# A gated-delta recurrence with raw keys: key norms and beta as row factors of the decay matrices, the values and the last product

## The chip, the cores and the metric

The kernel runs on one core of a Trainium2 chip. Its time is the device time of one execution in microseconds; before the change it is 2602.99 us, the median of three runs (2598.48 to 2603.35). One core has five engines that run side by side, each with its own queue of instructions worked off in order: TensorE (PE; its weight loads are listed apart as PEld), VectorE (DVE), ScalarE (ACT), GpSimd (POOL) and SyncE (SP), which here only issues DMA transfers.

## The reference

One layer of a streaming encoder is computed for 2048 prompt frames and for 8 running streams of 16 frames, all of width 1024. Each stream of tokens goes through a normalization, a wide projection, two head groups side by side, an output projection and a gated feed-forward part. The change lies in group A, the gated delta rule with 4 heads of 128:

```
q = l2norm(silu(conv(q))) * 128 ** -0.5
k = l2norm(silu(conv(k)))            # l2norm(x) = x * rsqrt(sum(x * x) + EPS)
v = silu(conv(v))
beta = sigmoid(b),   g = -exp(A_log) * softplus(a + dt_bias),   G = cumsum(g) inside a chunk
A    = strict_lower((beta_i k_i . k_j) * exp(G_i - G_j))
u, w = solve (I + A) [u | w] = [beta v | beta k exp(G)]
v_new = u - w S
o     = (q exp(G)) S + (lower(q . k) * exp(G_i - G_j)) v_new
S     = S * exp(G_last) + (k exp(G_last - G))^T v_new
```

`o` is normalized by head afterwards and gated with SiLU(z). All of it is float32.

## The kernel before

The tokens are 17 tiles of 128: 16 of the prompt, each of which is one chunk of the recurrence, and one (tile 16) that holds the 8 sample streams. They go through the first phase in six groups of two or three tiles:

```
GROUPS = [[0, 1, 16], [2, 3, 4], [5, 6, 7], [8, 9, 10], [11, 12], [13, 14, 15]]
```

The later phases (output projection, feed-forward) work on all tiles again and are not touched. For each group the first phase does, in program order: `x_prep` (rows normalized, split into a rounded part `hi` and a remainder `lo`; `x_first` for the first group); `gate_prep` (b and a projected; from them `sb`, `eG`, `tl`, `eL` and per tile the decay matrix `dt`); `qkv_stage`; `pair_stage`; `level_stage`; `z_stage`; one `chunk_stage` per prompt tile (`sample_stage` for tile 16); `sc_stage` (head group B).

A projection (`project`, line 352) of one block of 128 channels is 24 matmuls of 128x128 by 128x384 into one PSUM bank of the `psd` pool: 8 blocks of the contraction times three products of hi and lo parts (`mm3`, line 139). Its weights come by `fetch` and `weights`: in the first group they are cast on ScalarE (342) and the remainder is made by GpSimd or VectorE (344); later they are mostly read back, already split, as 1 MB transfers.

In `qkv_stage` the projections come out channel-major. `conv_qkv` moves the bank to SBUF (374 or 376), makes the four taps (401 or 403 on ScalarE, 370 on VectorE) and applies SiLU (405, 407). Then, per head:

- Keys: the tile is transposed to token-major in a bank of the `pst` pool, which has two (427); ScalarE squares and sums each row (412); `rstd` makes the inverse norm with a VectorE operation (131) and a power on GpSimd (133); VectorE multiplies it by `sb`, the square root of beta (430), and scales the keys with it while it copies them out of the bank (431), into `kt`. `kt` is then transposed back to channel-major in another `pst` bank (435) and copied by ScalarE into `kT` (437). So `kt` and `kT` both hold sqrt(beta) k / |k|.
- Values: transposed (444) and scaled by `sb` on the way out of the bank (445), into `vt`.
- Queries: `qT` is the channel-major SiLU itself; a transposition (452) only serves to sum the squares `ssq`, with which `out_stage` corrects the normalization of the output.

`pair_stage` forms k^T k and k^T q per head (519, 520) and multiplies both by `dt` (523 into `AU`, 524 in place into `dt`, from then on named QK). `AU` is written to memory in blocks of 32 and the 32x32 triangles are inverted by 31 steps of two VectorE operations each (539, 541); `level_stage` merges the blocks into `U`, the inverse for the 128 rows. `chunk_stage` forms the right-hand side from `kT`, the state, `eG` and `vt` (625 to 628), multiplies by `U` (632) into `yt`, scales `kt` by `tl` on GpSimd (636), and updates state (639, 642) and output (646 to 652).

Nothing of the order is written out by hand: a planner, which models the time of every instruction, writes the order of each engine's queue. Work of one group's recurrence is interleaved with the projections of the next. The tiles `kT`, `qT`, `kt`, `vt` lie in two pools that the groups use in turn; `kraw` and `vraw` share a ring of three buffers.

## Time and profile before

| | before |
|---|---|
| median of three runs | 2602.99 us |
| profiled execution, its own time | 2609.88 us |
| its span | 2608.1 us |
| granted TensorE clock, mean | 0.987 |
| busy in the span: PE, PEld, DVE, ACT, POOL | 2509.2, 2337.4, 1748.9, 1033.2, 645.1 us |
| instructions | 41962 |

A profile is one execution. Its busy times are sums over an engine's instructions; matmuls overlap, so TensorE's busy time is not its limit. Rows of groups give line, engine, operation, output and inputs with their shapes, the count, then the busy time in us and the mean in ns of one, and after the second bar the idle time of the engine just before them and what ended it. The chain of waits is followed back from the last instruction: at each step to what released it, or to the instruction before it on its engine. Rows of stretches give the busy time of each engine in a part of the span.

### The profile page before, as it was taken

Reading aid. Unit: us, or ns where it says so; the run is one execution under the profiler, and the core shown is the slowest. Engines: PE = TensorE matmul, PEld = TensorE weight load, DVE = VectorE, ACT = ScalarE, POOL = GpSimd, SP = SyncE. Lnnn points to the kernel's source line nnn. Section 1 sums busy time; section 2 is a strip of 40 time slices with the busy share of each in tenths; the row PEclk is TensorE's granted clock in tenths of the full one; section 3 lists DMA queues with packets and bytes.
Section 4 is the critical chain, followed back from the end, with each engine's and each line's share of the span. In section 5 each row is a group of like instructions: output and inputs, shape, how many; then the busy total and the mean of one; then the engine's idle time right before and its main releaser. Section 6 shows DMA issues by size and latency. Waiting matters only on the chain.

```text
span 2608.1 us, 41962 instructions
## 1 busy us (share of the span) xinstructions
PE 2509.2 (96%) x15129; PEld 2337.4 (90%) x15129; DVE 1748.9 (67%) x3549; ACT 1033.2 (40%) x2496; POOL 645.1 (25%) x598
## 2 busy tenths in 40 slices
PE   8989999999989999999999999999999999999998
PEld 7989899999888988778999999999999988788786
DVE  7787766666587665777878864544655555677598
ACT  6545144261554423444434442222433335333343
POOL 3321101010120101214556620000000025555563
PEclk9999999999999999999999999999999999999999
DMA  7876575757567573768877788887988853443466
GB/s 266 297 267 238 193 268 198 246 193 237 193 205 247 184 233 129 234 216 287 291 253 271 264 281 259 280 246 244 295 272 296 275 176 106 125 125 122 128 216 185
DMA packets 320816, 589.42 MB, mean 226 GB/s; under 512 B 55533, under 2 KB 204721, under 8 KB 301793
## 3 DMA queue, kind: packets, MB, share of 16 engines
q1 hardware_dynamic: 182512, 509.28, 58.8%
q10 hardware_dynamic: 138096, 77.46, 9.8%
q8 instruction: 120, 1.97, 0.3%
q14 instruction: 88, 0.71, 0.1%
HBM read 424.60 MB, written 162.05 MB: 225 GB/s over the span
## 4 chain that ended last, share of the span: by engine, by line
PE 70%; DVE 11%; DMA 9%; ACT 4%; issue 3%; POOL 2%; ACTq 1%; SPq 0%; DVEq 0%; POOLq 0%
PE fbank L1010 32%; PE dbank L139 15%; PE fbank L1168 10%; PE tbank L794 3%; PE dbank L794 3%; DMA xk<-in_xT 1%; DVE xr L1187 1%; DMA dr<-in_w_dn 1%; DVE acc L370 1%; DMA xt<-in_x 1%; DVE acc L1127 1%; DMA w<-wsplit 1%; DVE Ts L541 1%; DMA partd<-pt 1%; DMA utd<-sT 1%
## 5 line engine op out<-in xcount | busy, mean ns | idle before, releaser
L1010 PE MATMUL fbank<-xh,fw 128*128 128x384 f32 (+1 forms) x3696 | 901.3, 327 | 9.4 <-ACT m L1044 4.4
L139 PE MATMUL dbank<-hi,w 128*128 128x384 f32 (+1 forms) x2688 | 685.3, 334 | 12.7 <-ACT w L342 6.0
L1010 PEld LDWEIGHTS fbank<-xh,fw 128*128 128x128 f32 x3696 | 653.2, 188 | 11.3 <-ACT m L1044 5.0
L1010 PE MATMUL fbank<-xl,fw 128*128 128x384 f32 (+1 forms) x1848 | 603.7, 327 | 0.0
L139 PEld LDWEIGHTS dbank<-hi,w 128*128 128x128 f32 x2688 | 480.8, 191 | 18.5 <-ACT w L342 6.0
L1168 PE MATMUL fbank<-dw,as 128*128 128x512 f32 x1980 | 458.8, 393 | 8.6 <-DVE acc L1127 2.5
L1168 PEld LDWEIGHTS fbank<-dw,as 128*128 128x128 f32 x1980 | 370.6, 188 | 96.5 <-DVE acc L1127 4.5
L139 PE MATMUL dbank<-lo,w 128*128 128x384 f32 (+1 forms) x1344 | 446.4, 332 | 1.1 <-DVE lo L228 1.1
L1010 PEld LDWEIGHTS fbank<-xl,fw 128*128 128x128 f32 x1848 | 348.1, 188 | 0.0
L139 PEld LDWEIGHTS dbank<-lo,w 128*128 128x128 f32 x1344 | 256.9, 191 | 3.7 <-DVE lo L228 1.7
L1152 POOL TENSOR_TENSOR as<-ar,as 128x256 fp32r<-128x256 f32 (+1 forms) x207 | 186.5, 911 | 277.7 <-ACT as L1149 276.9
L1127 DVE TENSOR_TENSOR acc<-acc,fbank 128x512 f32<-128x512 f32 x248 | 166.3, 682 | 93.4 <-PE fbank L1168 75.6
L867 POOL TENSOR_TENSOR dw<-dr,dw 128x512 fp32r<-128x512 f32 x52 | 77.3, 1498 | 484.6 <-ACT dw L865 484.4
L1149 ACT CAST as<-ar 128x256 fp32r<-128x256 f32 (+1 forms) x288 | 117.8, 427 | 181.3 <-PE fbank L1168 130.0
L985 ACT CAST fw<-rg 128x512 fp32r<-128x512 f32 x124 | 77.3, 623 | 188.9 <-PE fbank L1010 170.8
L370 DVE SCALAR_TENSOR_TENSOR acc<-R,cw,acc 128x384 f32<-128x384 f32 (+2 forms) x216 | 132.8, 620 | 12.8 <-ACT acc L401 8.8
L344 POOL TENSOR_TENSOR w<-wr,w 128x512 fp32r<-128x512 f32 x49 | 73.0, 1490 | 228.0 <-ACT w L342 170.5
L1057 DVE TENSOR_TENSOR c<-u,fbank 128x384 f32<-128x384 f32 (+1 forms) x66 | 34.9, 529 | 102.2 <-PE fbank L1010 102.0
L1053 DVE TENSOR_TENSOR m<-m,m 128x384 f32<-128x384 f32 (+1 forms) x44 | 23.1, 525 | 97.8 <-ACT m L1046 97.8
L539 DVE TENSOR_TENSOR pr<-As,Ts 48x31 f32<-48x31 f32 (+25 forms) x186 | 66.7, 359 | 29.8 <-DMA As<-sa 25.7
L342 ACT CAST w<-wr 128x512 fp32r<-128x512 f32 x98 | 56.4, 616 | 61.9 <-PE dbank L139 29.4
L1055 ACT ACTIVATE m<-fbank 128x384 f32<-128x384 f32 (+1 forms) x66 | 31.2, 473 | 121.5 <-PE fbank L1010 112.4
(358 smaller groups left out, 3708.3 us busy)
## 6 DMA issues: line engine op xcount, KB each, us to landing
w<-wsplit SPq DMA_DIRECT2D x119, 1024.0 KB, 5.3
fw<-fsplit SPq DMA_DIRECT2D x188, 512.0 KB, 4.8
fsplit<-fw SPq DMA_DIRECT2D x94, 512.0 KB, 4.0
partd<-pt ACTq DMA_DIRECT2D x88, 384.0 KB, 6.5
rg<-in_w_gu SPq DMA_DIRECT2D x62, 512.0 KB, 4.3
wsplit<-w SPq DMA_DIRECT2D x28, 1024.0 KB, 5.3
wr<-in_w_in SPq DMA_DIRECT2D x98, 256.0 KB, 3.9
ar<-partd SPq DMA_DIRECT2D x48, 384.0 KB, 3.3
```

What stands on the lines that cost most here:

```text
L139: T.matmul(ps, l, r, start=(i == 0), stop=(i == n - 1))
L344: e.tensor_tensor(out=wl[:, c], in0=wr, in1=wh[:, c].bitcast(F32), op=ALU.subtract)
L370: V.scalar_tensor_tensor(acc, raw(d), w[:, d:d + 1], acc, op0=ALU.mult, op1=ALU.add)
L539: V.tensor_mul(p3, As[:m, j, j + 1:32].unsqueeze(2).broadcast_to([m, a, b]), Ts[:m, j, 0:b].unsqueeze(1).broadcast_to([m, a, b]))
L794: T.matmul(pss[n], m_[:, j, :], w_[k][:, n * 512:(n + 1) * 512], start=(k == 0 and ci == 0), stop=(k == KD - 1 and ci == 2))
L867: e.tensor_tensor(out=w[:, 1], in0=v, in1=w[:, 0].bitcast(F32), op=ALU.subtract)
L985: A.copy(w[:, 0], v)
L1010: T.matmul(ps, w_[:, c], b_[k][:, :hw], start=(first and k == 0 and ci == 0), stop=(k == KH - 1 and ci == 2), skip_group_check=not first)
L1127: V.tensor_add(dst, dst, ps)
L1149: ins = A.copy(a[:, 0, :n], v)
L1152: e.tensor_tensor(out=a[:, 1, :n], in0=v, in1=a[:, 0, :n].bitcast(F32), op=ALU.subtract)
L1168: T.matmul(ps, a[:, x_, q * P:(q + 1) * P], w[:, y_], start=(start and q == 0 and ci == 0), stop=(q == c - 1 and ci == 2), skip_group_chec ...
```

## The change

The inverse norms and beta are taken out of the keys. With s = sum of squares + EPS, the kernel now works with raw keys after SiLU:

- `kT` is the channel-major SiLU output itself (written straight into the pool's tile instead of the ring), and `kt` is its transposition, copied out of the bank by ScalarE. The second transposition, the `rstd` of each key head and its two multiplications by VectorE go.
- The sums of squares of all four heads are collected in one tile `ssk`, and once per group `c2` = beta / s is made on VectorE and `rt` = s ** 0.5 by one power on GpSimd (with a constant 0.5 in a new tile `half`).
- `beta` is now exp(-softplus(-b)) where `sb` was its square root (scale -1.0 instead of -0.5 in line 285).
- The values are scaled by `rt` instead of `sb` (same instruction and shape).
- `tl`, the factors of `kt` in the last product, is multiplied by `c2` (one operation per group).
- Each decay matrix `dt` is multiplied per head by the column of `c2` of its tile on ScalarE: four multiplications of 128x128 per tile, placed after a value head.

`sumsq` now writes into a tile that is handed to it.

```diff
--- before.py
+++ after.py
@@ -125,6 +125,8 @@
     g_hd = vec[:, 16:17]
     neghalf = const.tile([P, 4 * MAXT], F32, name="neghalf")
     V.memset(neghalf, -0.5)
+    half = const.tile([P, 4 * MAXT], F32, name="half")
+    V.memset(half, 0.5)
 
     def rstd(small, ss, n, scale, eps, tag):
         m = small.tile([P, n], F32, tag=tag + "m", name=tag + "m")
@@ -282,7 +284,7 @@
             sp3 = sp.rearrange("p (t c) -> p t c", c=8)
             sb, gg, nG, eG, tl, eL = (sm(nm) for nm in ("sb", "gg", "nG", "eG", "tl", "eL"))
             v3 = lambda a: a.rearrange("p (t h) -> p t h", h=H)
-            A.activation(v3(sb)[:, :n], sp3[:, :n, 0:4], AF.Exp, scale=-0.5)
+            A.activation(v3(sb)[:, :n], sp3[:, :n, 0:4], AF.Exp, scale=-1.0)
             V.tensor_mul(v3(gg)[:, :n], sp3[:, :n, 4:8], nega.unsqueeze(1).broadcast_to([P, n, H]))
             ps = bank() if rb is not None else tbank()
             q = 4 * npr
@@ -321,7 +323,7 @@
                                            neg_s if t == SAMPLE else neg_p, op0=ALU.add, op1=ALU.add)
                 A.activation(dt, dt, AF.Exp)
                 dts.append(dt)
-            return dict(sb=sb, eG=eG, tl=tl, eL=eL, eLs=eLs, dt=dts)
+            return dict(beta=sb, eG=eG, tl=tl, eL=eL, eLs=eLs, dt=dts)
 
         wloads = []
         stores = []
@@ -406,36 +408,35 @@
             if npr < n:
                 A.activation(dst[:, pc:c].rearrange("p (s l) -> p s l", s=NS), segments(acc, pc, 0, 3 + LS)[:, :, 3:], AF.Silu)
 
-        def sumsq(ps, n, nm):
-            ss = small.tile([P, n], F32, tag=nm, name=nm)
+        def sumsq(ps, n, ss):
             for i in range(n):
-                A.activation(junkq, ps[:, i * P:(i + 1) * P], AF.Square, accum_out=ss[:, i:i + 1])
-            return ss
+                A.activation(junkq, ps[:, i * P:(i + 1) * P], AF.Square, accum_out=ss(i))
 
         def qkv_stage(tiles, hi, lo, rb, gt, pool):
             n = len(tiles)
             c = n * P
+            m = 4 * n
             kt = pool.tile([P, H, MAXT, P], F32, tag="kt", name="kt")
             vt = pool.tile([P, H, MAXT, P], F32, tag="vt", name="vt")
+            ssk = small.tile([P, 4 * MAXT], F32, tag="ssk", name="ssk")
             kT, qT, ssq = [], [], []
-            sb = gt["sb"].rearrange("p (t h) -> p t h", h=H)
             for h in range(H):
-                raw = cp.tile([P, W1], F32, tag="kvT", name="kraw", bufs=NKV)
-                conv_qkv(tiles, 4 + h, project(h, hi, lo, c), raw, rb)
+                o = pool.tile([P, W1], F32, tag="kT", name="kT", bufs=H)
+                conv_qkv(tiles, 4 + h, project(h, hi, lo, c), o, rb)
                 ps = tbank()
                 for i in range(n):
-                    T.transpose(ps[:, i * P:(i + 1) * P], raw[:, i * P:(i + 1) * P], ident)
-                ss = sumsq(ps, n, "ssk")
-                rk = rstd(small, ss, n, 1.0, EPS, "rk")
-                V.tensor_mul(rk, rk, sb[:, :n, h])
-                V.tensor_mul(kt[:, h, :n], ps[:, :c].rearrange("p (t d) -> p t d", d=P),
-                             rk.unsqueeze(2).broadcast_to([P, n, P]))
-                ps = tbank()
-                for i in range(n):
-                    T.transpose(ps[:, i * P:(i + 1) * P], kt[:, h, i, :], ident)
-                o = pool.tile([P, W1], F32, tag="kT", name="kT", bufs=H)
-                A.copy(o[:, :c], ps[:, :c])
+                    T.transpose(ps[:, i * P:(i + 1) * P], o[:, i * P:(i + 1) * P], ident)
+                sumsq(ps, n, lambda i: ssk[:, 4 * i + h:4 * i + h + 1])
+                A.copy(kt[:, h, :n], ps[:, :c].rearrange("p (t d) -> p t d", d=P))
                 kT.append(o)
+            c2 = small.tile([P, 4 * MAXT], F32, tag="c2", name="c2")
+            rt = small.tile([P, 4 * MAXT], F32, tag="rt", name="rt")
+            V.tensor_scalar_add(ssk[:, :m], ssk[:, :m], EPS)
+            G.tensor_tensor(out=rt[:, :m], in0=ssk[:, :m], in1=half[:, :m], op=ALU.pow)
+            V.reciprocal(c2[:, :m], ssk[:, :m])
+            V.tensor_mul(c2[:, :m], c2[:, :m], gt["beta"][:, :m])
+            V.tensor_mul(gt["tl"][:, :m], gt["tl"][:, :m], c2[:, :m])
+            rt3 = rt.rearrange("p (t h) -> p t h", h=H)
             for h in range(H):
                 raw = cp.tile([P, W1], F32, tag="kvT", name="vraw", bufs=NKV)
                 conv_qkv(tiles, 8 + h, project(4 + h, hi, lo, c), raw, rb)
@@ -443,14 +444,19 @@
                 for i in range(n):
                     T.transpose(ps[:, i * P:(i + 1) * P], raw[:, i * P:(i + 1) * P], ident)
                 V.tensor_mul(vt[:, h, :n], ps[:, :c].rearrange("p (t d) -> p t d", d=P),
-                             sb[:, :n, h].unsqueeze(2).broadcast_to([P, n, P]))
+                             rt3[:, :n, h].unsqueeze(2).broadcast_to([P, n, P]))
+                if h < n:
+                    for g in range(H):
+                        A.mul(gt["dt"][h][:, g, :], gt["dt"][h][:, g, :], c2[:, 4 * h + g:4 * h + g + 1])
             for h in range(H):
                 o = pool.tile([P, W1], F32, tag="qT", name="qT", bufs=H)
                 conv_qkv(tiles, h, project(8 + h, hi, lo, c), o, rb)
                 ps = tbank()
                 for i in range(n):
                     T.transpose(ps[:, i * P:(i + 1) * P], o[:, i * P:(i + 1) * P], ident)
-                ssq.append(sumsq(ps, n, f"ssq{h}"))
+                ss = small.tile([P, MAXT], F32, tag=f"ssq{h}", name=f"ssq{h}")
+                sumsq(ps, n, lambda i: ss[:, i:i + 1])
+                ssq.append(ss)
                 qT.append(o)
             gt.update(kt=kt, vt=vt, kT=kT, qT=qT, ssq=ssq)
 
```

## The prediction

> **What bounds the kernel now.** I read the page first, then the stretches of 25 us, then TensorE's waits, and the single instructions last.
>
> ```profile
> span 2608.1 us, 41962 instructions
> PE 2509.2 (96%) x15129; PEld 2337.4 (90%) x15129; DVE 1748.9 (67%) x3549; ACT 1033.2 (40%) x2496; POOL 645.1 (25%) x598
> ```
> ```profile
> PE 70%; DVE 11%; DMA 9%; ACT 4%; issue 3%; POOL 2%; ACTq 1%; SPq 0%; DVEq 0%; POOLq 0%
> ```
>
> TensorE is busy 96% of the span and carries 70% of the chain that ended last. So an instruction taken off TensorE is worth its time, and one taken off another engine is worth only the wait that it ends. The edit lies in the recurrence's phase, so the stretches of that phase come next. The columns are the stretch, its length, the busy time of PE, PEld, DVE, ACT and POOL (with counts), the granted clock, the DMA share and GB/s.
>
> ```profile
> 0.00:1050.00 1050.00, 989.86 (x6937) 933.35 (x6937) 711.47 (x1892) 454.21 (x1212) 153.43 (x156) 0.98 0.67 224
> ```
> ```profile
> 150.00:175.00 25.00, 16.84 (x82) 15.11 (x82) 21.45 (x61) 6.13 (x12) 6.16 (x5) 0.80 0.91 310
> 175.00:200.00 25.00, 25.00 (x240) 22.78 (x239) 15.55 (x48) 21.83 (x48) 2.70 (x4) 1.00 0.57 212
> ...
> 400.00:425.00 25.00, 24.70 (x168) 24.23 (x168) 18.68 (x55) 14.53 (x44) 5.00 (x5) 1.00 0.62 208
> ```
>
> In the first 1050 us TensorE is idle for 1050 - 989.9 = 60 us. The worst stretch is the handover from the first group to the second (16.8 of 25 busy). Where key and value heads of a later group run (400 to 425) TensorE is full, while ScalarE has 25 - 14.5 = 10.5 us free and the DMA share is 0.62, so neither sets the pace there. TensorE's waits in this phase, with the total, the times and the longest:
>
> ```profile
> PE tbank L139 <- ACT hi L209: 12.0, 4, 8.0
> ...
> PE tbank L435 <- DVE kt L431: 4.3, 6, 2.5
> PE tbank L452 <- ACT junkq L412: 3.6, 3, 2.2
> ```
>
> The second row is the transposition that the edit removes: it waits for the normalized keys.
>
> **The change part by part.** *Term A, the transpositions.* Line 435 goes, 68 of them (17 tiles by 4 heads).
>
> ```profile
> L435 PE MATMUL tbank<-cst,kt 128*128 128x128 f32 x68 | 12.3, 276 | 4.3 <-DVE kt L431 4.3
> ```
> ```profile
> 169.44 1.92 PE dbank L139 x6
> ...
> 187.10 4.39 PE dbank L139 x24
> ...
> 211.01 0.33 PE tbank L435 x3
> ```
>
> One takes 276 ns, but they overlap: in the chain three of them take 0.33 us, 0.11 each. The lower price is 68 x 0.11 = 7.5 us; the upper is the 12.3 us of busy time, which contains the pipeline's tails that other matmuls overlap. I take 7.5, because the chain counts each stretch of time once.
>
> *Term B, their waits.* The 4.3 us before line 435 go with it if nothing else is late at the same place, and stay whole if the next instruction is. Next in line is the transposition of another head's keys or values, which after the edit waits only for a SiLU and for a transposition bank. That bank is freed sooner too: by the three squares and a copy, without the way over VectorE, GpSimd and VectorE again. Of 0 to 4.3 I take 3.
>
> *Term C, the handover from the first group to the second.* These rows are from the timelines of TensorE, ScalarE and VectorE.
>
> ```profile
> 93.08 0.52 PE L435 MATMUL tbank<-cst,kt 128*128 128x128 f32 x3 [0.18 <-DVE kt L431]
> ```
> ```profile
> 92.23 0.42 ACT L405 ACTIVATE qT<-acc 128x256 f32<-128x256 f32 x1 [1.24 <-DVE acc L370]
> ```
> ```profile
> 164.52 0.18 DVE L541 TENSOR_TENSOR Ts<-Ts,pr 48x31 f32<-48x31 f32 x1
> ...
> 166.10 1.01 DVE L206 TENSOR_TENSOR xk<-xk,rb 128x384 f32<-128x384 f32 x2
> ```
>
> The last head's keys are transposed again only at 93.1, and the pair matrices need all heads. The long solve on VectorE that comes out of them ends at 164.7, and the next group's rows follow at 166.1, for which TensorE waits 8.0 us. The edit lets the keys through earlier and takes about 4 us of work from VectorE in each group (below), but the last queries get their SiLU at 92.2 as well, so the pair matrices can't come much sooner. The bounds are 0 and 8.0 plus the slow start behind the wait: six matmuls of line 139 take 1.92 us there (0.32 each), 24 take 4.39 later (0.18 each). If 6 to 8 of them ran slow, that is 6 to 8 x 0.14 = about 1, so 9 us. I take 2, near the lower end, because the queries are as late as the keys.
>
> [...]
>
> *Term D, VectorE and GpSimd.*
>
> ```profile
> L431 DVE TENSOR_TENSOR kt<-tbank,rkr 128x384 f32<-128x384 f32 (+1 forms) x24 | 12.7, 531 | 0.3
> L430 DVE TENSOR_TENSOR rkr<-rkr,sb 128x3 f32<-128x3 f32 (+1 forms) x24 | 6.8, 285 | 5.1 <-POOL rkr L133 4.7
> L131 DVE TENSOR_SCALAR rkm<-ssk 128x3 f32<-128x3 f32 (+1 forms) x24 | 5.0, 209 | 12.0 <-ACT junkq L412 12.0
> ...
> L278 DVE RECIPROCAL ru<-uu 128x24 f32<-128x24 f32 (+1 forms) x6 | 1.7, 286 | 0.0
> L307 DVE TENSOR_TENSOR tl<-tbank,nG 128x12 f32<-128x12 f32 (+1 forms) x5 | 0.8, 168 | 5.6 <-ACT eL L306 5.6
> ```
> ```profile
> L133 POOL TENSOR_TENSOR rkr<-rkm,neghalf 128x3 f32<-128x3 f32 (+1 forms) x24 | 23.5, 979 | 120.4 <-DVE rkm L131 98.4 <-DVE R L391 13.7 <-DVE hist L393 8.2
> ```
>
> VectorE loses 12.7 + 6.8 + 5.0 = 24.5 us and gets per group a reciprocal (0.29) and three small operations (0.17 each): 6 x 0.8 = 4.8. GpSimd does 6 powers instead of 24: 23.5 becomes about 6. Neither is the bound, so D is 0 beyond what C holds; the added clearing of a small constant lies ahead of all this and is 0 too.
>
> *Term E, ScalarE.* The copy of the second transposition (line 437) becomes a copy of the first, the same in number and shape: 0. New are 68 multiplications of 128x128 by a column; no row shows one in SBUF. The nearest rows:
>
> ```profile
> L412 ACT ACTIVATE junkq<-tbank 128x128 bf16<-128x128 f32 x136 | 37.4, 275 | 37.2 <-PE tbank L452 15.2 <-DVE o L652 5.8 <-PE dbank L139 3.6
> ...
> L401 ACT ACTIVATE acc<-dbank,cw 128x384 f32<-128x384 f32 x48 | 28.2, 587 | 0.1
> ...
> L437 ACT COPY kT<-tbank 128x384 f32<-128x384 f32 x20 | 9.5, 473 | 10.5 <-PE tbank L435 10.3
> ```
>
> The shape alone gives 275 ns. A column factor adds 587 - 473 = 114, so 389 is the upper price: 18.7 to 26.5 us in all, and 12 x 0.39 = 4.7 in a group of three tiles. I take the upper one, as the operand is a column. The cover is ScalarE's 10.5 us of idle time per 25 in those stages. On the path I put 1 us for it, out of 0 to 26.5. Queued behind a multiplication on ScalarE are the evacuations and SiLUs of the next heads, for which VectorE's taps and TensorE's banks wait; it has itself only the squares and two or three small VectorE operations to wait for, and the exponentials that were made earlier on the same engine.
>
> *Term F, the new wait.* The values are now multiplied by the key norms, so the first of them waits for all four key heads and for the one power. In the third group:
>
> ```profile
> 409.94 0.33 PE tbank L427 x3
> ...
> 420.57 0.33 PE tbank L444 x3
> ```
>
> The last keys are transposed 10.6 us before the first values. Three squares (0.8), their reads (no more than that again), an addition (0.2) and a power (1.0) take 2.8 us at most, so the wait is covered by nearly 8 us. That cover is gone if the power stands in GpSimd's queue behind a blocked product of the recurrence:
>
> ```profile
> POOL kl L636 <- PE gbank L639: 52.7, 9, 15.2
> ```
>
> Its longest wait is 15.2 us; behind that, the values would come 15.2 + 2.8 - 10.6 = 7.4 us late, less the time that the second bank gives (one projection, 4.4 by the 24 matmuls above): about 3 us in a group, 15 in five. I take 0.
>
> *The sum.* 7.5 + 3 + 2 - 1 = 11.5 us. The profiled execution took 2609.88 us (span 2608.1 and 1.8 around it), so it would be 2598.4. The median of the three runs is 2602.99, 6.9 below the profiled one; taken off the median, the forecast is 2591.5. Unknown beyond this is the planner: it writes every engine's order anew from modelled times. The trace bounds its luck by what the same handover costs in different places: 8.0 us once, (12.0 - 8.0) / 3 = 1.3 on average elsewhere, so up to about 6.
>
> **The rivals.** *Larger:* B and C come whole. 7.5 + 4.3 + 9 = 20.8, 2582. For it speaks that keys leave the first group's late chain; against it that the queries stay. *No change:* the freed time comes back as waits, above all term F, or as a handover made worse by the planner's 6 us: 11.5 less 6 to 15, about 2600. For it speaks the row of line 636; against it that GpSimd has less to do and the values lie 10 us behind. *Slower:* ScalarE becomes the bound around the values and queries. Place: the multiplications stand ahead of the next heads' evacuations and SiLUs. It decides where ScalarE has less than 4.7 us free in its stretch, that is above about 20 of 25, as at 175 to 200 (21.8). Price: up to 26.5 on the path against 7.5 + 3 + 2 = 12.5, so up to +14; at three quarters, 19.9 - 12.5 = +7, 2610. Against it: in the key and value stage above it stands at 14.5. [...] *Not what it says* is hard to see: the diff drops lines 434 and 435 outright.
>
> **How the numbers follow.** The forecast has 0.60, its own range 2583 to 2597 (the sum at 20 to 6); the larger gain 0.10; no change 0.17; slower 0.13. About 0.2%, 5 us, is what a measurement can tell from no change. So faster is 0.60 + 0.10 = 0.70, same 0.17, slower 0.13. The range is 2579 (the larger gain and 3 us of the planner's) to 2606: it takes in no change and leaves out most of slower.
>
> **What would show it.** Right: no row of line 435, TensorE's matmuls fewer by 68, VectorE's busy time about 20 us lower, GpSimd's 17, ScalarE's some 20 to 26 higher; TensorE's idle time in the first 1050 us lower by a few us. Wrong: waits of the value transpositions for their scaled product or of that product for the power (F); of TensorE for ScalarE's evacuations in the value and query stages (E); a longer wait for the next group's rows (C or the planner).

## The result, and the profile after

The changed kernel takes 2627.35 us (median of four runs, 2621.65 to 2629.62); the kernel before takes 2603.17 us (median of four runs, 2598.48 to 2605.61; three of them are the runs of the table at the start). The ratio is 1.0075, with a 95% interval of 1.0049 to 1.0100. The forecast was a gain of 11.5 us; the kernel became about 20 us slower by the ratio (24 by the two medians), and the time lies above the range. Beside the experiments below the kernel before took 2607.7 to 2611.4 us; set against these, the 2627.35 us of the change are 0.6 to 0.75% slower.

First the page of the changed kernel: the span, the busy times of the engines, and the shares of the chain that ended last. (These add up to 58%: the chain was followed no further back, and does not reach the recurrence.)

```profile
span 2625.3 us, 41826 instructions
PE 2518.9 (96%) x15061; PEld 2345.7 (89%) x15061; DVE 1744.6 (66%) x3502; ACT 1057.0 (40%) x2567; POOL 632.9 (24%) x580
PE 46%; DVE 6%; DMA 2%; issue 2%; POOL 1%; ACT 1%; ACTq 0%; SPq 0%; DVEq 0%; POOLq 0%
```

TensorE has 15061 matmuls where it had 15129: exactly 68 fewer. Yet its busy time went *up*, from 2509.2 to 2518.9 us. Fewer instructions with more busy time means that some of those that stayed ran slower. The granted clock says the same (view of the cores, first the kernel before, then the changed one):

```profile
core 0: 2608.1 us, clock 0.987
```
```profile
core 0: 2625.3 us, clock 0.979
```

In the records of both kernels this clock has only two values, 1 and 0.5. So the time at half clock is twice what is missing to 1: 2 x 0.013 x 2608.1 = 68 us before, 2 x 0.021 x 2625.3 = 110 us after, 42 us more. The profiled execution of the changed kernel has the lowest clock of its four (the others 0.981 to 0.983), so the 42 us are rather too much than too little.

Where in the program? The source view of the first matmul line of the feed-forward part (the same matmuls, line 1010 before and 1016 after; the columns are count, ns of one at three quantiles, and first start to last) gives the length of all that lies ahead of it:

```profile
L1010 PE MATMUL fbank<-xh,fw x3696: 303/334/522, 1198.9 to 2128.0; 128*128 128x384 f32 x130, 128*128 128x320 f32 x65
```
```profile
L1016 PE MATMUL fbank<-xh,fw x3696: 302/334/689, 1214.4 to 2144.2; 128*128 128x384 f32 x130, 128*128 128x320 f32 x65
```

It starts 1214.4 - 1198.9 = 15.5 us later, and the span ends 17.2 us later. So nearly all of the loss arises ahead of the feed-forward part. The stretches of the changed kernel there (length, then busy time of PE, PEld, DVE, ACT, POOL with counts, clock, DMA share, GB/s):

```profile
0.00:1050.00 1050.00, 985.24 (x6809) 930.51 (x6810) 699.03 (x1839) 477.91 (x1282) 141.99 (x137) 0.97 0.65 222
50.00:75.00 25.00, 22.15 (x113) 21.31 (x114) 17.35 (x46) 19.36 (x51) 8.47 (x6) 0.80 0.58 198
975.00:1000.00 25.00, 21.41 (x134) 18.46 (x131) 16.11 (x29) 12.08 (x21) 2.48 (x2) 0.74 0.64 211
```

Both of the 25 us stretches had a full clock before, the first of them the one in which the first group's keys and values run:

```profile
50.00:75.00 25.00, 21.91 (x133) 20.95 (x132) 19.16 (x56) 17.42 (x44) 8.62 (x7) 1.00 0.78 265
...
975.00:1000.00 25.00, 25.00 (x137) 21.32 (x136) 18.64 (x36) 11.98 (x26) 4.61 (x4) 1.00 0.59 180
```

After, TensorE is as busy at 50 to 75 us (22.2 against 21.9) but gets through 113 matmuls instead of 133, at a clock of 0.80. In neither stretch is another engine busy throughout (at most 19.4 of 25 us), so it isn't seen there that one of them became the bound for good. Shorter stretches of the changed kernel show how the clock falls:

```profile
49.50:52.90 3.40, 1.88 (x15) 1.88 (x15) 1.25 (x5) 3.35 (x10) 1.27 (x1) 1.00 0.01 2
52.90:56.30 3.40, 2.58 (x9) 1.98 (x9) 2.84 (x9) 3.36 (x10) 0.00 (x0) 0.50 0.70 255
56.30:59.70 3.40, 2.39 (x9) 2.39 (x10) 0.98 (x5) 3.29 (x15) 1.09 (x1) 0.50 0.57 207
59.70:63.10 3.40, 3.40 (x13) 3.30 (x12) 1.85 (x6) 2.70 (x7) 2.47 (x2) 0.50 0.00 0
```
```profile
51.02 0.55 PE L428 MATMUL tbank<-cst,kT 128*128 128x128 f32 x3 [1.73 <-ACT kt L430]
...
57.31 0.90 PE L445 MATMUL tbank<-cst,vraw 128*128 128x128 f32 x3 [1.55 <-ACT kt L430]
```

In the second view, TensorE's timeline, a number in square brackets is the wait ahead of an instruction, with what ended it. TensorE is kept waiting 1.73 us before a key transposition and 1.55 us before a value transposition, both times for the copy of a key head out of its bank, which stands in a ScalarE that is full (3.35 of 3.4 us). The clock falls after the first of the two waits and is 0.5 from 52.9 to 63.1 us; the second wait lies inside.

To say what share each of these has, I reckon every kernel of this case in the same way, from its TensorE records. Each matmul is given as *work* the usual distance from its start to the next start (the 30th percentile of its line and shape over all runs). *Gaps* is the time from its end to the next start. What remains inside the stretches at half clock is the *half-clock loss*, what remains elsewhere the *rest*; some 19 us at the two ends belong to none. The level of the half-clock loss depends by about 6 us on how the matmuls are grouped for their usual distance (another grouping gives 22.3 and 38.4 us for the two kernels below), the difference of two kernels by one to three. In microseconds of the profiled execution:

| | work | gaps | half-clock loss | rest | span |
|---|---|---|---|---|---|
| before | 2420.9 | 80.3 | 28.0 | 60.0 | 2608.1 |
| after | 2412.8 | 87.6 | 45.0 | 60.7 | 2625.3 |
| difference | -8.1 | +7.3 | +17.0 | +0.7 | +17.2 |

The 8 us of the transpositions are gained, as forecast. About the same amount comes back as gaps, and 17 us more are lost because TensorE runs 42 us longer at half clock.

### The profile page after: what moved, and what is told of

Its sections match the earlier page's. It is cut to its first block, busy times and chain, and to the rows that moved or that the text cites. A ratio compares the mean times of both kernels' runs of the same rounds, so it can differ in the third digit from the quotient of the medians.

```text
span 2625.3 us, 41826 instructions
## 1 busy us (share of the span) xinstructions
PE 2518.9 (96%) x15061; PEld 2345.7 (89%) x15061; DVE 1744.6 (66%) x3502; ACT 1057.0 (40%) x2567; POOL 632.9 (24%) x580
## 4 chain that ended last, share of the span: by engine, by line
PE 46%; DVE 6%; DMA 2%; issue 2%; POOL 1%; ACT 1%; ACTq 0%; SPq 0%; DVEq 0%; POOLq 0%
PE fbank L1016 33%; PE fbank L1174 11%; PE tbank L800 1%; PE dbank L800 1%; DVE xr L1193 1%; DVE acc L1133 1%; DMA partd<-pt 1%; POOL dw L873 1%; DMA dr<-in_w_dn 1%; DVE as L1158 0%; DMA fh<-hTd 0%; DVE dw L873 0%; DVE acc L1190 0%; DVE xl L944 0%; DVE fw L992 0%
## 5 line engine op out<-in xcount | busy, mean ns | idle before, releaser
L873 POOL TENSOR_TENSOR dw<-dr,dw 128x512 fp32r<-128x512 f32 x52 | 76.8, 1490 | 486.0 <-ACT dw L871 485.7
L545 DVE TENSOR_TENSOR pr<-As,Ts 48x31 f32<-48x31 f32 (+25 forms) x186 | 63.6, 342 | 26.4 <-DMA As<-sa 22.1
```

The lines of the kernel that those rows point to most:

```text
L545: V.tensor_mul(p3, As[:m, j, j + 1:32].unsqueeze(2).broadcast_to([m, a, b]), Ts[:m, j, 0:b].unsqueeze(1).broadcast_to([m, a, b]))
L873: e.tensor_tensor(out=w[:, 1], in0=v, in1=w[:, 0].bitcast(F32), op=ALU.subtract)
```

## The experiments

**Three theories.** *S*: the load that the change adds on ScalarE (68 multiplications, and the copies of the keys that wait behind them) holds up TensorE's banks; without it the kernel would be faster than before. *P*: the planner writes all orders anew after any edit; the order it had found for the kernel before falls well, those for the changed kernel fall worse, and the edit's own work hardly matters. *C*, which goes with either: short gaps cost more than their length, because a stretch of short gaps and tiny matmuls brings the clock down, as it seems to from 52.9 us above (1.88 of 3.4 us busy, no gap longer than 1.73 us, then a clock of 0.50).

Each experiment gives a ratio to the kernel before with its 95% interval and the terms of the same reckoning.

### Without the multiplications, and with nothing but them

The first leaves out the multiplications of the decay matrices by `c2` (in the changed kernel they are line 450) and puts a constant -5 into the masks in their place, so that the numbers stay in a similar size; part of the computation is left out. The second adds the same 68 multiplications, by a column of ones, to the kernel before.

```diff
 # e1_no_scale, against the changed kernel
-                if h < n:
-                    for g in range(H):
-                        A.mul(gt["dt"][h][:, g, :], gt["dt"][h][:, g, :], c2[:, 4 * h + g:4 * h + g + 1])
 # e2_before_plus_scale, against the kernel before
+                if h < n:
+                    for g in range(H):
+                        A.mul(gt["dt"][h][:, g, :], gt["dt"][h][:, g, :], ones[:, 4 * h + g:4 * h + g + 1])
```

> The changed kernel without the 68 multiplications of the decay matrices on ScalarE (line 443 of it). It leaves the factors beta / |k|^2 out of the decay matrices; a constant of -5 in the exponent's mask keeps the solve bounded, with the same instructions. Theory S (ScalarE's new work is the burden): most of the 24 us comes back, so 2600 to 2608, and TensorE's time at half clock falls from 108 us towards the 67 us of the kernel before. Theory P (the planner writes a new order for any edit, and how its gaps fall is luck): the time may go either way by some 10 us, with no relation to ScalarE's busy time; near 2620 is as likely as 2600. Theory C (small gaps in TensorE's work cost double, since they halve its clock for the windows behind them) says only that time follows matmul work plus gaps plus the loss at half clock, in this run as in the others.

> The kernel before with 68 multiplications of the decay matrices on ScalarE added behind its value heads, at the same place as in the change, by a column of ones, so that the output stays the same. Theory S: slower by most of the change's loss plus what the transpositions saved, some 20 to 32 us, so 2623 to 2635. Theory P: anything from -10 to +15 us, about 2593 to 2618, and the same size as for an edit without weight.

| | ratio [95%] | work | gaps | half-clock loss | span |
|---|---|---|---|---|---|
| e1_no_scale | 1.0024 [1.0012, 1.0036] | 2412.5 | 88.6 | 37.2 | 2617.5 |
| e2_before_plus_scale | 1.0028 [1.0012, 1.0044] | 2420.9 | 85.9 | 40.3 | 2625.1 |

Without the multiplications the changed kernel is still slower than before, with the gaps of the whole change (88.6 against 87.6 us). With them alone the kernel before loses 0.28%. Together that is 0.52%, less than the 0.75% of the change. The median of e2, 2618.19 us, lies below the 2623 to 2635 us that S said; its profiled execution, 2626.85 us, is the slowest of seven, so the row shows it at its worst. But e1 is what speaks most against S: the kernel with 68 matmuls and 47 VectorE instructions fewer and nothing on ScalarE but squares and copies as before is 0.24% slower.

### The keys' copy on VectorE; the second transposition gone alone

In e3 the changed kernel's copy of the transposed keys is VectorE's instead of ScalarE's. In e4 the kernel before loses its second transposition and nothing else: the raw keys serve as `kT`, without a factor (computation left out; -5 in the masks and in `tl` in place of the factors), while norms, `kt`, values and queries stay as they were.

```diff
 # e3_kt_dve
-                A.copy(kt[:, h, :n], ps[:, :c].rearrange("p (t d) -> p t d", d=P))
+                V.tensor_copy(kt[:, h, :n], ps[:, :c].rearrange("p (t d) -> p t d", d=P))
 # e4_before_no_second
-                raw = cp.tile([P, W1], F32, tag="kvT", name="kraw", bufs=NKV)
+                raw = pool.tile([P, W1], F32, tag="kT", name="kT", bufs=H)
...
-                ps = tbank()
-                for i in range(n):
-                    T.transpose(ps[:, i * P:(i + 1) * P], kt[:, h, i, :], ident)
-                o = pool.tile([P, W1], F32, tag="kT", name="kT", bufs=H)
-                A.copy(o[:, :c], ps[:, :c])
-                kT.append(o)
+                kT.append(raw)
```

> The changed kernel with the copy of the token-major keys out of the bank on VectorE, as before, in place of ScalarE. Theory S (ScalarE's load): the copies (11 us) leave ScalarE, the two waits of TensorE for that copy in the first group go, and the time falls by a few us, to about 2615 to 2622 beside 2627. Theory P (the planner's order decides, and with it where gaps and half-clock windows fall): anything between 2605 and 2630. Theory C (time follows matmul work plus gaps plus loss at half clock) has to hold in the trace either way.

> The kernel before with the second transposition and its copy alone left out: the channel-major keys stay raw, the token-major ones are normalized as before. What it leaves out is the norm and beta in one of the two copies of the keys; two constants of -5 in exponents keep the numbers bounded, with as many instructions. It has the saving of the change and none of its additions, and ScalarE has 11 us less to do. The prediction's terms A and B: 7.5 to 11.8 us faster, 2591 to 2596. Theory P: the 8 us of matmul time are saved for certain, but gaps and half clock move by luck, so 2580 to 2610, and a time above 2603 would speak for it alone.

| | ratio [95%] | work | gaps | half-clock loss | span |
|---|---|---|---|---|---|
| e3_kt_dve | 1.0033 [1.0020, 1.0047] | 2413.5 | 87.1 | 39.0 | 2617.0 |
| e4_before_no_second | 1.0030 [1.0018, 1.0042] | 2413.6 | 82.9 | 40.4 | 2612.1 |

e4 is the purest form of the idea: work is taken away and none is put in its place. It gets its 7.3 us of work (2420.9 to 2413.6) and is 0.30% slower all the same, through 12.4 us more of half clock in its profile (gaps +2.6, the rest -3.6). In its waits of TensorE in the first 1050 us (total, times, longest) there is no line of a key transposition any more:

```profile
PE dbank L139 <- DMA w<-wsplit: 8.1, 7, 2.4
PE tbank L139 <- ACT hi L209: 8.0, 1, 8.0
PE tbank L179 <- DVE rg L176: 7.4, 2, 6.8
```

Other waits stand there, and the order is another one. Compared by the sequence of source lines on TensorE ahead of the feed-forward part, e4's order matches that of the kernel before in a share of 0.51, the changed kernel's in 0.48. Such a share depends on the way of matching (others give 0.55 to 0.78 for the kernels compared here), so only its distance from 1 is used.

The copy on ScalarE, that ended the two waits shown above, isn't the only cause of the lost clock in the first group: e3 has no such copy and e4 no ScalarE work that was not there before, and a half-clock stretch stands at 57 to 64 us in the one and at 54 to 61 in the other. The time of e3 (2616.89 us) decides nothing, as it lies in what S said, 2615 to 2622 us, and in what P said.

### The same work elsewhere

Three kernels move the multiplications of the changed kernel: to GpSimd (e7) and to VectorE (e8), one instruction per tile instead of four, and, in a_fold, into the exponent, where nothing is multiplied: the logarithm of `c2` is added to `nG` and the decay matrices are made after the key heads.

```diff
 # e7_scale_pool (e8_scale_dve: V.tensor_mul with the same operands)
-                    for g in range(H):
-                        A.mul(gt["dt"][h][:, g, :], gt["dt"][h][:, g, :], c2[:, 4 * h + g:4 * h + g + 1])
+                    G.tensor_tensor(out=gt["dt"][h], in0=gt["dt"][h], in1=bc(c2[:, 4 * h:4 * h + 4]), op=ALU.mult)
 # a_fold
+            A.activation(lc[:, :m], c2[:, :m], AF.Ln)
+            V.tensor_add(gt["nG"][:, :m], gt["nG"][:, :m], lc[:, :m])
+            gt["decay"]()
```

> The changed kernel with the decay matrices scaled by GpSimd, one instruction of 128x512 per tile (17 in all, about 1.15 us each by the row of line 636), in place of 68 on ScalarE. Theory S: ScalarE falls back by its 20 to 26 us, and the time to that of the run without the scaling, about 8 us above the kernel before in the same call, unless VectorE is held up by it. Theory P: anything within 10 us of that.

> The same with the scaling on VectorE, 17 instructions of 128x512, about 0.75 us each by the row of line 612, 13 us in all. Theory S: like the run with GpSimd, since VectorE still has less to do than before; about 6 to 10 us above the kernel before. Theory P: anything within 10 us of that.

> The changed kernel without the 68 multiplications: the logarithm of beta / |k|^2 is added to the column that goes into the exponent of the decay matrices, which are made after the key heads (one logarithm and one addition of 128x12 per group). Nothing is left out of the computation. Theory S: as the run without the scaling, 0.24% above the kernel before, less if its order is kind. Theory P: 0 to 0.7% above, without relation to ScalarE.

| multiplications on | ratio [95%] | gaps | half-clock loss | span |
|---|---|---|---|---|
| ScalarE, 68 (the change) | 1.0075 [1.0049, 1.0100] | 87.6 | 45.0 | 2625.3 |
| GpSimd, 17 (e7) | 1.0063 [1.0045, 1.0082] | 93.8 | 35.8 | 2621.0 |
| VectorE, 17 (e8) | 1.0045 [1.0028, 1.0062] | 90.3 | 40.5 | 2621.4 |
| none, in the exponent (a_fold) | 1.0063 [1.0047, 1.0079] | 87.9 | 42.8 | 2623.0 |
| none, left out (e1) | 1.0024 [1.0012, 1.0036] | 88.6 | 37.2 | 2617.5 |

The groups of instructions give their price, in the changed kernel, in e7 and in e8 (busy time, ns of one, then idle time ahead):

```profile
L450 ACT ACTIVATE dt<-dt,c 128x128 f32<-128x128 f32 x68 | 20.8, 388 | 0.2 <-DVE c L437 0.2
```
```profile
L449 POOL TENSOR_TENSOR dt<-dt,c 128x512 f32<-128x512 f32 x17 | 19.1, 1142 | 5.8 <-DMA xt<-in_x 4.4 <-ACT dt L324 1.4
```
```profile
L449 DVE TENSOR_TENSOR dt<-dt,c 128x512 f32<-128x512 f32 x17 | 13.1, 806 | 0.0
```

From 20.8 us on ScalarE to nothing on any engine, the ratios show no relation with the load: a_fold, which multiplies nothing, is as slow as e7 and within the interval of the change. S had put a_fold at the 0.24% of e1, and e7 and e8 at about 6 to 10 us above the kernel before, where they lie at some 16 and 12; it falls. What all five share is raw keys, and orders that are not that of the kernel before.

### Edits without work

If P holds, an edit that does nothing should move the time as well. e5 clears 12 columns on VectorE once per group in the kernel before, e6 copies 12 columns on ScalarE; nobody reads the result.

```diff
+            nop = small.tile([P, 12], F32, tag="nop", name="nop")
+            V.memset(nop, 0.0)              # e5_before_dve_nop
+            A.copy(nop, ones[:, 0:12])      # e6_before_act_nop
```

> The kernel before with one VectorE memset of 128x12 more in each of the six groups, about 0.1 us each and read by nobody. Theory S: no change, within 2 us of 2603. Theory P: the planner's order differs and the time with it, by 5 us or more in one of the two directions, with gaps and half-clock time moved by as much.

> The kernel before with one ScalarE copy of 128x12 more in each of the six groups (about 0.2 us each), read by nobody. Theory S: no change, within 2 us of the kernel before. Theory P: as VectorE's idle instruction gave no change, this one tells whether a small edit on ScalarE, whose order decides when banks are free, does: 5 us or more either way if it does.

e5: 0.9998 [0.9989, 1.0007]; e6: 1.0003 [0.9988, 1.0018]. No change, which looked like a blow to P. But the order on TensorE matches that of the kernel before in a share of 0.997 and 0.993: the planner put the small instructions in and left all else. The two runs show that an edit without effect on the order has none on the time, and nothing on what another order costs. They also show how far two executions of nearly one order differ in the reckoning: e5 has 80.1 us of gaps, e6 75.8, and half-clock losses some 4 and 5 us below that of the kernel before. Smaller differences in these tables say nothing.

So two exchanges followed that do the same work in another order, made alike in the kernel before (b) and in the changed one (a). In *qv* the query heads come before the value heads, with the weights' order to match; in *zl*, `z_stage` comes before `level_stage` in the loop over the groups.

```diff
 # b_qv, a_qv: query loop ahead of the value loop, and
-        order = [(j, gi) for gi in range(len(GROUPS)) for j in range(28)]
+        order = [(j, gi) for gi in range(len(GROUPS)) for j in (*range(4), *range(8, 12), *range(4, 8), *range(12, 28))]
 # b_zl, a_zl: the call of level_stage moves behind that of z_stage
-            level_stage(tiles, gt)
...
+            level_stage(tiles, gt)
```

> The kernel before with the four query heads ahead of the four value heads in each group (order of the weights and of the stage alike). No instruction is added or removed, but the planner's order on TensorE differs widely, which it did not with the two idle instructions. Theory P (the order of the kernel before falls well, and any edit that gives another order loses that): slower by 0.2 to 0.7%, with the matmul work as before and the loss at half clock up by 8 to 17 us. Theory S (the change pays for work that it adds): within 0.2% of the kernel before.

> The changed kernel with the query heads ahead of the value heads. Theory P: about as far above or below the changed kernel's 0.75% as luck has it, 0 to 0.8% above the kernel before, and within 0.4% of the kernel before with the same exchange. Theory S: 0.5 to 0.8% above the kernel before with the same exchange; the value transpositions, which wait for the key norms, come later, so that wait (the prediction's term F) can't be what costs.

> The kernel before with the z stage's four projections ahead of the level stage in program order; again no instruction added or removed and another order on TensorE. Theory P: slower by 0.2 to 0.7% through gaps and half clock. Theory S: within 0.2%.

> The changed kernel with the same exchange of z stage and level stage. Theory P: 0 to 0.8% above the kernel before, within 0.4% of the kernel before with that exchange. Theory S: 0.5 to 0.8% above the kernel before with that exchange.

| | ratio [95%] | work | gaps | half-clock loss | span |
|---|---|---|---|---|---|
| b_qv | 1.0063 [1.0041, 1.0086] | 2421.7 | 93.7 | 35.7 | 2626.6 |
| a_qv | 1.0062 [1.0043, 1.0081] | 2412.9 | 94.1 | 40.6 | 2625.0 |
| b_zl | 1.0013 [1.0000, 1.0026] | 2421.5 | 83.9 | 29.7 | 2612.6 |
| a_zl | 1.0026 [1.0012, 1.0040] | 2413.3 | 90.4 | 34.2 | 2615.3 |

b_qv computes what the kernel before computes, with the same number of matmuls, and loses 0.63%: 13.4 us more of gaps and 7.7 of half clock. Its order matches in a share of 0.57, that of b_zl in 0.51. With *qv* the kernels with and without the change are equal (1.0063 and 1.0062); with *zl* they differ by 0.13%, where S had put the changed one 0.5 to 0.8% above the other in both. For b_zl itself P missed: it had said 0.2 to 0.7%, and 0.13% is what S said, too. In the waits of b_qv the normalized keys, gone in the change, stand with 9.0 us where they had 4.3:

```profile
PE tbank L139 <- ACT hi L209: 10.2, 2, 8.9
PE tbank L435 <- DVE kt L431: 9.0, 7, 4.4
PE dbank L139 <- DMA w<-wsplit: 8.7, 5, 2.8
```

So another order of the same work can cost about as much as the change lost (0.63% with an interval of 0.41 to 0.86, against 0.75%), and the order of the kernel before leaves only 4.3 us of waits for the keys' second pass. This is what P says of b_qv; that the order is also what the change itself lost by is likely from the equal pair, but not shown apart from raw keys.

### The planner without its model of times

The planner can also order the work without its model of times. That was done with both kernels.

```diff
-TLS = True
+TLS = False
```

> The kernel before with the planner's time model off, so that its order follows the program and priorities and not modelled times. It serves as the base of the next run. Its own time may be well above 2603; no theory gives a number.

> The changed kernel with the planner's time model off. Against the kernel before with the model off: theory S (the change's own load on ScalarE and its waits) says slower by 10 to 25 us; theory P (only the modelled order spoils it) says faster, by the 8 us of matmul work and up to some 10 us of waits less, since the order of both is nearly the same.

| | median | ratio to before [95%] | work | gaps | half-clock loss | rest | span |
|---|---|---|---|---|---|---|---|
| b_tls0 | 2779.13 us | 1.0650 [1.0586, 1.0715] | 2420.3 | 170.7 | 116.7 | 71.8 | 2797.2 |
| a_tls0 | 2744.3 us | 1.0513 [1.0444, 1.0582] | 2413.4 | 170.3 | 74.1 | 80.8 | 2755.6 |

Here the change *is* faster: 2744.3 / 2779.13 = 0.987; taken from the ends of the two intervals, 1.0444 / 1.0715 to 1.0582 / 1.0586, that is 0.975 to 1.000 at the widest. The two longest waits of TensorE in the first 1200 us, first without, then with the change:

```profile
PE tbank L435 <- DVE kt L431: 14.6, 15, 3.2
PE obank L615 <- DVE o L612: 10.5, 10, 2.1
```
```profile
PE tbank L141 <- ACT hi L211: 10.9, 4, 4.1
PE obank L621 <- DVE o L618: 10.5, 10, 2.1
```

In an order that isn't fitted to the kernel, the second transposition waits 14.6 us for the normalized keys, 15 times, and that goes. The two orders are also much nearer to each other than those of the kernel before and of the change: matched by tiles, without the removed transposition, they agree in a share of 0.92, the latter two in 0.59. But the total of the gaps stays (170.7 and 170.3 us), as other waits take the place; the half-clock loss falls by 42.6 us, against which the rest grows by 9. So the 6.9 us of work are gained as the prediction thought, and most of the gain comes through the clock, for which its sum has no term. By the medians the gain is 34.8 us, more than the 18 that P had said at most. Both profiled executions took longer than the medians (2799.30 and 2757.44 us), so their half-clock losses are rather too large. That the planner with its model had covered most of this already fits the 4.3 us of waits there, but is an argument.

### Searching for a better order of the changed kernel

Three more kernels of the changed work: a ring of two raw tiles instead of three and five row buffers instead of four (xkb5), and *zl* with that or with the copy of e3.

```diff
 # a_xkb5, a_zl_xkb5
-NR, NKV = 3, 3
-XKB = 4
+NR, NKV = 3, 2
+XKB = 5
```

> The changed kernel with a ring of two instead of three buffers for the values (the keys no longer use it) and one buffer more for the next group's rows. Theory P: another order, 0 to 0.8% above the kernel before. If the wait at the handover between groups is what the change loses at, this run is near the kernel before or under it.

> The changed kernel with the z stage ahead and the fifth row buffer (two buffers for the values). Adding up 0.49 and 0.39 points it would be 0.1% faster than the kernel before. Theory P: 0 to 0.7% slower.

> The changed kernel with both the z stage ahead of the level stage and the key copy on VectorE. If the gains of the two edits add up (0.75 - 0.26 = 0.49 and 0.75 - 0.33 = 0.42 points), it is 0.1 to 0.2% faster than the kernel before. Theory P: they do not add up; 0 to 0.7% slower again.

| | ratio [95%] | gaps | half-clock loss | span |
|---|---|---|---|---|
| a_xkb5 | 1.0036 [1.0021, 1.0052] | 85.5 | 40.1 | 2618.0 |
| a_zl_xkb5 | 1.0032 [1.0015, 1.0049] | 84.9 | 32.8 | 2608.7 |
| a_zl_kt | 1.0039 [1.0023, 1.0055] | 87.3 | 36.3 | 2613.9 |

Alone, *zl*, xkb5 and e3 each took 0.4 to 0.5% off the change; together they take no more than one of them. So they are no parts of a cost that add up, which P had said. No version was faster than the kernel before.

### What stays open

The kernel before and the two with idle instructions are the best of all runs with the planner's model; the two other orders of the same work lie at +0.13% and +0.63%, and e2, with the multiplications added, at +0.28%. The twelve kernels with raw keys, the change and e4 among them, lie between +0.24% and +0.75%. With two other orders of the work before, I can't exclude that raw keys themselves cost one or two tenths of a per cent under this planner. Nor is it shown *why* its orders are worse in the first group. There all twelve kernels with raw keys start projection 12 (counted from 0, the first behind those of keys, values and queries) at 82.1 to 84.8 us, and the kernels before, e5 and e6 at 77.1 to 77.2. Raw keys aren't needed for this delay: b_qv, with normalized keys, starts it at 84.9 us, b_zl at 76.8 and e2 at 78.3. That the long normalization of the keys had made the planner put projections in between, which covered all that came later, is an argument from reading the two orders, not a result.

## Why the prediction was wrong

**Term A, the transpositions (7.5 us).** Right: 68 matmuls gone, 8.1 us of work, taken from starts to starts. In the planner-off pair it is 6.9, in e4 7.3; as the reckoning gives the same matmul the same time everywhere, this spread is its own error. The 30th percentile of the distance from one of these transpositions to the next start is 0.109 us over all runs, and 68 of that are 7.4.

**Term B, the waits ahead of line 435 (4.3, taken as 3).** The rows went and others came, so it gave nothing: the key, value and query transpositions had 10.5 us of idle time ahead of them before (1.7, 4.3, 0.9 and 3.6 us) and have 12.8 after (7.4, 3.6 and 1.8). The groups of the first and the value transposition in the changed kernel have, after the second bar, the new idle time:

```profile
L428 PE MATMUL tbank<-cst,kT 128*128 128x128 f32 x68 | 12.4, 294 | 7.4 <-DVE tl L309 5.7 <-ACT kt L430 1.7
L445 PE MATMUL tbank<-cst,vraw 128*128 128x128 f32 x68 | 12.2, 287 | 3.6 <-ACT kt L430 1.8 <-DVE vt L446 1.8
```

These two have 11.0 us, where I had said that the next transposition waits only for a SiLU and for a bank. It waits for a bank indeed, but that bank is held by the gates' `tl` (5.7 us) or by the copy of the keys: the order now puts the transposition where its bank is taken. The prediction had named this bound (nothing gained, if something else is late at the same place) and valued it at 1.3 of 4.3 us.

**Term C, the handover from the first group to the second (0 to 9, taken as 2).** Wrong in sign. The waits of TensorE in the first 1050 us of the changed kernel:

```profile
PE tbank L141 <- ACT hi L211: 11.1, 3, 9.7
PE dbank L141 <- ACT w L344: 6.3, 2, 6.1
PE tbank L428 <- DVE tl L309: 5.7, 3, 3.0
PE obank L621 <- DVE Ts L547: 3.9, 1, 3.9
```

The longest wait for the next group's rows grew from 8.0 to 9.7 us (the total of these waits fell from 12.0 to 11.1). The keys did lose their second pass, but the first group reached projection 12 at 83.3 us where it had been at 77.2: the order, not the removed work, set the time there.

**Term D, VectorE and GpSimd (0).** Right in effect. The sizes were off: VectorE's busy time fell by 4.3 us over the span (12.4 in the first 1050), not 20; GpSimd's by 12.2, not 17, as the one power for four heads took more than twice as long as that for one head (2293 against 979 ns):

```profile
L435 POOL TENSOR_TENSOR rt<-ssk,half 128x12 f32<-128x12 f32 (+1 forms) x6 | 13.8, 2293 | 64.8 <-DVE ssk L434 33.3 <-DVE R L393 27.0 <-DMA wr<-in_w_in 4.5
```

**Term E, the multiplications on ScalarE (389 ns each, 1 us on the path).** The estimate met the 388 ns of the row above, and ScalarE's busy time rose by 23.8 us. The sum of 26.5 us was too high all the same: the 68 multiplications are busy for 20.8 us together, 0.31 each, as those behind one another overlap (293 ns from start to start, 388 from start to end). What they cost on the path can't be read off: without them (e1) the kernel is 0.51% faster than with them, yet with the same factor in the exponent and no multiplication (a_fold) only 0.12%. The rival *Slower* gave the right sign, its price (+7) was about a third of the loss, and its mechanism, ScalarE as the bound around values and queries, isn't what the runs show: that place lost nothing that moving the work away would bring back.

**Term F, the wait of the values for the power (0).** Right. The value transposition waits 1.8 us once for `vt`, which had waited 1.7 us for the power:

```profile
L446 DVE TENSOR_TENSOR vt<-tbank,rt 128x384 f32<-128x384 f32 (+1 forms) x24 | 12.4, 528 | 1.8 <-POOL rt L435 1.7
```

**The steps that failed.** Two. The first is the bound on the planner, "up to about 6" us, worked out from how much one handover's wait differed from place to place in *one* order. The runs put another order at up to 0.63% with the same work, some 16 us. The second is the clock, for which the sum has no term. I had priced each wait at its length (those of line 435 were 2.5 us at the longest) and each order at the sum of such prices. In the changed kernel a wait of 1.73 us stands right ahead of a fall of the clock that lasts 10.2 us, and one of 1.55 us inside it. The trace of the kernel before spoke against such prices already: it has 11 stretches at half clock, the shortest of 3.41 us, and only three gaps longer than 3.4 us (7.98, 3.48 and 4.09). The 17.0 us more of half-clock loss, in a span that is 17.2 us longer, are in none of them. That another order alone raises the half-clock loss is shown by b_qv (7.7 us more with the same work); whether the 17 us of the change are its order's doing alone stays open. Behind both stands the choice of baseline: the kernel before was priced as if it were an average order of its work, and it is the best one seen.

## What to carry to other kernels

Where a planner writes the queues, the time before belongs to one order, and an edit that takes work away also throws that order away; before believing a gain or a loss below 1%, make an exchange that changes the order and not the work, make sure by comparing the orders that it really did, and take its spread as the error of the edit. Reckon TensorE's time as work, gaps and time at half clock (twice what the mean clock lacks to 1, times the span, where its records have only the values 1 and 0.5, as here): in this case the last moved more than the other two. A latency that the order already hides is worth nothing to remove; the same edit was 1.3% faster, for the larger part through the clock, in an order that didn't hide it.

## What the runs showed of the hardware that I had not expected

**Short waits with tiny matmuls between them were followed by half the clock.** Without the one at the end, the changed kernel has 17 stretches at half clock (99 us) where there were 11 (58 us), each of them about 3.4 us or a multiple of it, and only three gaps longer than 3.4 us (9.72, 3.86 and 4.03 us). In the rows of 49.5 to 63.1 us above, TensorE is busy for 1.88 of the 3.4 us ahead of the fall, with no gap longer than 1.73 us, and for 3.40 of 3.4 us before the clock is back; between the wait of 1.73 us and the fall lie eight matmuls with 8 or 4 columns (lines 292 to 297, from 52.28 us). So 3.4 us in which TensorE was busy for more than half of the time were followed by the half clock. How busy it was ahead of each fall can be read from the traces. The half-clock stretches begin and end on a grid of 3.41 us. Leave out the two ends of the span: of the steps of this grid at full clock, all 28 that end in a fall (11 before, 17 after) have TensorE busy for at most 1.99 us, and one of them has no gap longer than 0.51 us; those after which the clock stays full are busy for at least 1.66 us. In the traces of all twenty kernels no step with less than 1.49 us kept the clock and none with more than 2.92 us lost it. So in these records, in which the ends of matmuls are modelled, the clock went with the busy time of a step, and no gap as long as a step was needed. No sharp limit shows: between 1.66 and 1.99 us of 3.41 in the two kernels, and between 1.49 and 2.92 in all twenty, a step can stand on either side. The price: the matmuls of 128x384 of line 141 start 320 ns apart at half clock and 173 ns at the full one (medians of the changed kernel), so by this ratio 42 us more at half clock lose up to 42 x (1 - 173 / 320) = 19 us, an estimate; 17 were lost.

**A GpSimd power took longer with more columns:** 979 ns for 128x3 (line 133 before) and 2293 ns for 128x12 (line 435 after; means in which a few smaller ones are mixed). I had reckoned with the same 1.0 us for both.

**ScalarE by a column factor** took 388 ns for 128x128, where three rows of the kernel before had given an estimate of 275 + 587 - 473 = 389. That those behind one another start 293 ns apart, and the 68 are busy for 20.8 us and not 26.4, I had not expected.
